# Sliding-window attention: two key blocks folded into one block of 128 columns

## The chip, the cores and the metric

The kernel runs on one core of one Trainium2 chip. The time is what the device takes for one execution, in microseconds (us); three runs of the kernel before gave a median of 1572.53, from 1572.28 to 1574.33. Each engine of the core works through its own queue in order: PE multiplies matrices (PEld loads its weights), DVE and ACT are the vector and the scalar engine, POOL is a second, general engine, and SP issues most DMAs. They wait for each other by semaphores.

## The reference, cut to what matters

One decoder block over 1024 positions of 1024 features: norm, one combined projection, a retention branch and an attention branch in parallel, a gated merge, then a feed-forward part. The change is in the attention branch: 16 query heads of 64 features, 2 key/value heads, a window of 128 positions, and one learned sink logit for each head.

```python
kb = jnp.concatenate([kp[:, :-1], kp[:, 1:]], axis=2)   # the block before, and the block itself
vb = jnp.concatenate([vp[:, :-1], vp[:, 1:]], axis=2)
scores = jnp.einsum('bnqhgd,bnkhd->bnhgqk', qb, kb).astype(jnp.float32) * (d ** -0.5)
rel = C + qi - kj
mask = (rel[None] >= 0) & (rel[None] < WINDOW) & (key_pos >= 0)
scores = jnp.where(mask[None, :, None, None], scores, -1e30)
m = jnp.maximum(jnp.max(scores, axis=-1, keepdims=True), sink)
e = jnp.exp(scores - m)
probs = e / (jnp.sum(e, axis=-1, keepdims=True) + jnp.exp(sink - m))
out = jnp.einsum('bnhgqk,bnkhd->bnqhgd', probs.astype(v.dtype), vb)
```

With C = WINDOW = 128, query row i of a block sees the columns after i of the block before it, and the columns up to i of its own block: together exactly 128, and each column of 0 to 127 once, from one block or the other.

## The kernel before

All activations are held feature by feature in fp32r, most of them as a high and a low part, so that a product takes three matmuls (hi x hi, hi x lo, lo x hi). The attention stage runs from about 98 us to 335 us of the span and is cut into 32 units u = 8g + b: g is a group of four query heads, b a block of 128 queries. The keys stand negated and stacked in `kst`, the values in `vst`, with the high part in columns 0 to 63 and the low part in 64 to 127 of each block and key/value head; `av_evac` writes them from the projection's two halves.

A unit has three parts. `u_scores(u)` multiplies the queries with two key blocks (256 columns; one block for b = 0), two heads to a PSUM bank `s`. DVE adds the mask and takes the row minimum together with the sink in one operation (L464, the scores are negated), ACT takes the exponential with its sum (L467), DVE the reciprocal, and DVE and ACT scale two heads each (L475, L473). POOL copies the sink column into the score tile `sc` first (L452). `u_transpose(u)` transposes the four heads, key block by key block, on PE into banks `pT` (L485), and ACT and DVE write each bank's high part `ph` and low part `pl` (L488, L489). `u_values(u)` multiplies `vst` with `ph` and `pl` of each key block into the bank `pv` (L498, L499); ACT and DVE add the halves (L502 to L505) and write the result over the queries (L507, L508).

The loop at L528 goes through the units as a pipeline: transposes of unit i-1, scores of unit i, a share of other work, then values of unit i-1. The other work is a generator, `Fill`, of plain projections: the query projections of the next group (`quad_q`, tiles `aq`, `wh_aq`, `wl_aq`; rotary work L420 to L429 on DVE and ACT) and sigmoid gates (`gate`, tiles `acc_g`, `wh_g`, `wl_g`). After the last unit the rest of the fill runs (L553), and then the retention-value products begin (tiles `vP`, `va`).

Program order only sets priorities there: a scheduler writes each engine's queue from them, so instructions of units and fill stand in an order of its making, fixed when the program is built. `sc` has two buffers, `ph` and `pl` two, `pT` and `s` two banks each, `pv` one. In the blocks marked `in_order` (the norm ahead of the stage, the vector sums behind it) the order is that of the program.

Of the kernel before, what the change touches and what calls it, by code (L numbers as in the profile page):

```python
# [39 lines left out]
def hybrid_block(ctx: ExitStack, tc: tile.TileContext, x, ln1_g, w_in, b_in, ret_norm_g, w_ret_out,  # L40
# [261 lines left out]
    with tc.tile_pool(name="gt", bufs=1, side="right") as gt, tc.tile_pool(name="w1", bufs=1) as w1:  # L302
        atab = w1.tile([P, 2, S], F32, name="atab")
        nc.sync.dma_start(atab, c_atab.rearrange("z p s -> p z s"))
        amask = w1.tile([P, 256], F32, name="amask")
# [139 lines left out]
        def u_scores(u):  # L445
# [7 lines left out]
            nm = tiny.tile([P, 4], F32, tag="nm", name=f"nm{g}{b}")
            den = tiny.tile([P, 4], F32, tag="den", name=f"den{g}{b}")
            for jp in range(2):
                pt = ps("s", 2, f"s{g}{b}{jp}")
                for jj in range(2):
                    j = 2 * jp + jj
                    o = pt[:, jj * 256:jj * 256 + nk]
                    nc.tensor.matmul(o, Bt[:, jb + j, qc], kst[:, kv, 0, k0:k0 + nk], start=True, stop=False)  # L460
                    nc.tensor.matmul(o, Bt[:, jb + j, qc], kst[:, kv, 1, k0:k0 + nk], start=False, stop=True)  # L461
                for jj in range(2):
                    j = 2 * jp + jj
                    nc.vector.tensor_tensor_reduce(out=sc[:, j, 0:nk], in0=pt[:, jj * 256:jj * 256 + nk], in1=mk,  # L464
                                                   scale=1.0, scalar=nsink[:, 4 * g + j:4 * g + j + 1],
                                                   op0=ALU.add, op1=ALU.min, accum_out=nm[:, j:j + 1])
                    nc.scalar.activation(sc[:, j, 0:nk + 1], sc[:, j, 0:nk + 1], AF.Exp, scale=-1.0,  # L467
# [3 lines left out]
            for j in range(4):  # L471
                if j % 2:
                    nc.scalar.activation(sc[:, j, 0:nk], sc[:, j, 0:nk], AF.Copy, scale=rd[:, j:j + 1])  # L473
                else:
                    nc.vector.tensor_scalar(out=sc[:, j, 0:nk], in0=sc[:, j, 0:nk], scalar1=rd[:, j:j + 1],  # L475
                                            scalar2=None, op0=ALU.mult)

        def u_transpose(u):
            g, b, nk, Bt, jb, qc = geo(u)
            sc = scs.pop(u)  # L480
            phs[u] = []
            for kb in range(nk // P):
                pt = ps("t", 2, f"pT{g}{b}{kb}")
                for j in range(4):
                    nc.tensor.transpose(pt[:, j * P:(j + 1) * P], sc[:, j, kb * P:kb * P + P], ident)  # L485
# [2 lines left out]
                nc.scalar.copy(ph, pt)  # L488
                nc.vector.tensor_tensor(out=pl, in0=pt, in1=f32(ph), op=ALU.subtract)  # L489
                phs[u].append((ph, pl))  # L490

        def u_values(u):
            g, b, nk, Bt, jb, qc = geo(u)
            nkb = nk // P
            pv = ps("pv", 1, f"pv{g}{b}")
            for kb, (ph, pl) in enumerate(phs.pop(u)):
                vb = vst[:, b - nkb + 1 + kb, g // 2, :]
                nc.tensor.matmul(pv, vb, ph, start=(kb == 0), stop=False)  # L498
# [1397 lines left out]
```

## Time and profile before

The profile is of one execution, on its only core. In the views, a row gives line, engine, operation, out<-in by the program's names, shapes and count; then busy us and the mean ns of one; then the engine's idle time ahead of them and what ended it. Timeline rows begin with the start and the time taken, in us.

| | us |
|---|---|
| median of three runs | 1572.53 |
| the profiled execution, whole | 1574.62 |
| its span, first to last instruction | 1572.5 |
| attention stage in it | about 98 to 335 |
| granted TensorE clock, mean | 0.999 of full |

Matmuls overlap in PE's pipeline: a row's duration (389 ns for 512 columns) is longer than the spacing of two that follow each other, so that busy PE time is no measure of how much PE could still take.

### The profile page before, as it was taken

The page shows a single profiled execution, that of the slowest core. Times are in us where ns is not written, and L with a number is a line of the kernel's source. Part 1 is how long each engine was busy: PE and PEld are TensorE (multiplying, and loading weights), DVE is VectorE, ACT ScalarE, POOL GpSimd, SP SyncE. Part 2 cuts the span into 40 slices and gives each one's busy share as a digit, 9 for nine tenths or more (in the row PEclk, how much of TensorE's full clock was granted, in tenths as well). Part 3 has the DMA queues.
Part 4 walks back from the last instruction along what each step waited for, and adds up shares of the span by engine and source line. Part 5 has one row for each costly group of instructions (what it writes and reads, how often), then busy time and mean ns, then how long its engine had stood idle before and what let it go on. Part 6 is the DMA issues. An engine that isn't in the chain of part 4 may idle for free.

```text
span 1572.5 us, 20870 instructions
## 1 busy us (share of the span) xinstructions
PE 1559.8 (99%) x7435; PEld 1297.5 (83%) x7435; DVE 1016.6 (65%) x1809; ACT 732.5 (47%) x1460; POOL 381.8 (24%) x320
## 2 busy tenths in 40 slices
PE   9999999999999999999999999999999999999998
PEld 8887888888888888888888888888888888888886
DVE  6369978777657663787656879444444444678756
ACT  5258877844233334544223366333333333444445
POOL 2000000000045441000021123655555555100001
PEclk9999999999999999999999999999999999999999
DMA  6563754441374454765555502333333333863333
GB/s 203 155 178 118 217 181 148 160 135 41 101 236 148 137 170 164 240 202 165 163 187 186 187 1 78 113 114 105 101 101 106 106 110 101 291 250 84 98 102 126
DMA packets 152581, 228.36 MB, mean 145 GB/s; under 512 B 9307, under 2 KB 81821, under 8 KB 150942
## 3 DMA queue, kind: packets, MB, share of 16 engines
q1 hardware_dynamic: 152476, 227.04, 44.6%
q8 instruction: 58, 0.95, 0.2%
q14 instruction: 45, 0.37, 0.1%
q10 hardware_dynamic: 2, 0.00, 0.0%
HBM read 152.29 MB, written 69.99 MB: 141 GB/s over the span
## 4 chain that ended last, share of the span: by engine, by line
PE 89%; ACT 6%; DVE 3%; issue 1%; DMA 0%; POOL 0%; POOLq 0%; ACTq 0%; DVEq 0%
PE fA L1518 15%; PE fB L1518 8%; PE dA L1820 7%; PE wA L842 7%; PE dxP L1820 6%; PE fC L1518 4%; PE wB L842 3%; PE wo L1352 3%; PE va L687 3%; PE acc_g L158 2%; PE acc_g L159 2%; PE acc_g L160 2%; PE woP L1352 2%; PE vP L687 2%; ACT sc L467 2%; PE acc_ba L159 2%
## 5 line engine op out<-in xcount | busy, mean ns | idle before, releaser
L1820 PE MATMUL dA<-dwP,daP 128*128 128x512 f32 x528 | 120.6, 389 | 0.0
L1820 PEld LDWEIGHTS dA<-dwP,daP 128*128 128x128 f32 x528 | 99.0, 188 | 20.7 <-DVE dwP L134 0.2
L1820 PE MATMUL dxP<-dwP,daP 128*128 128x512 f32 x396 | 90.2, 389 | 0.0
L1820 PEld LDWEIGHTS dxP<-dwP,daP 128*128 128x128 f32 x396 | 74.3, 188 | 15.4
L452 POOL COPY sc<-nsink 128x4 f32<-128x4 f32 x32 | 13.2, 413 | 274.5 <-PE pT L485 157.2
L158 PE MATMUL acc_g<-h,wh_g 128*128 128x512 f32 x192 | 75.4, 393 | 0.1
L159 PE MATMUL acc_g<-h,wh_g 128*128 128x512 f32 x192 | 75.2, 392 | 0.0
L160 PE MATMUL acc_g<-h,wl_g 128*128 128x512 f32 x192 | 75.1, 393 | 0.0
L467 ACT ACTIVATE sc<-sc,nm 128x257 f32<-128x257 f32 (+1 forms) x128 | 62.5, 492 | 27.0 <-DVE nm L464 26.6
L1593 POOL TENSOR_TENSOR xf<-xf 128x512 f32<-128x512 f32 x40 | 64.5, 1611 | 30.3 <-issue 28.8
L1524 POOL TENSOR_TENSOR xf<-xf 128x512 f32<-128x512 f32 x33 | 47.3, 1435 | 58.7 <-ACT xf L1526 26.9
L464 DVE CUSTOM_DVE_ANT_0 sc<-s,amask,nsink 128x256 f32<-128x256 f32 (+1 forms) x128 | 54.0, 460 | 9.8 <-PE s L461 9.5
L134 DVE TENSOR_TENSOR dwP<-wd,dwP 128x512 fp32r<-128x512 f32 x77 | 52.6, 684 | 5.5 <-ACT dwP L131 5.5
L1725 POOL TENSOR_TENSOR rs_f<-tot,mhalf 128x1 f32<-128x1 f32 x8 | 4.9, 607 | 205.4 <-DVE tot L1722 205.4
L131 ACT CAST dwP<-wd 128x512 fp32r<-128x512 f32 x77 | 47.4, 616 | 9.3 <-PE dA L1820 7.1
L131 ACT CAST daP<-daP 128x512 fp32r<-128x512 f32 x42 | 26.0, 621 | 54.0 <-PE dxP L1820 26.7
L158 PE MATMUL acc_bb<-ay,wh_bb 128*128 128x512 f32 x128 | 51.1, 400 | 0.0
L556 POOL TENSOR_TENSOR wr_wp<-wr_wp 128x512 f32<-128x512 f32 x10 | 16.6, 1658 | 140.0 <-DVE w0P L134 122.5
L159 PE MATMUL acc_bb<-ay,wh_bb 128*128 128x512 f32 x128 | 50.3, 393 | 0.0
L160 PE MATMUL aq<-h,wl_aq 128*128 128x512 f32 x128 | 50.2, 392 | 0.0
L159 PE MATMUL aq<-h,wh_aq 128*128 128x512 f32 x128 | 50.2, 392 | 0.0
L158 PE MATMUL aq<-h,wh_aq 128*128 128x512 f32 x128 | 50.2, 392 | 0.0
(826 smaller groups left out, 4374.6 us busy)
## 6 DMA issues: line engine op xcount, KB each, us to landing
act_d<-xf SPq DMA_DIRECT2D x77, 256.0 KB, 2.1
daP<-act_d SPq DMA_DIRECT2D x21, 512.0 KB, 3.6
q_d<-stg SPq DMA_DIRECT2D x8, 1024.0 KB
q<-q_d SPq DMA_DIRECT2D x32, 256.0 KB, 6.2
ay_d<-q SPq DMA_DIRECT2D x8, 1024.0 KB
ay<-ay_d SPq DMA_DIRECT2D x4, 2048.0 KB, 14.2
wr_daP<-act_d SPq DMA_DIRECT2D x14, 512.0 KB, 6.4
wr_g<-in_w_in SPq DMA_DIRECT2D x12, 512.0 KB, 6.0
```

Source lines behind the costliest of these rows:

```text
L131: nc.scalar.copy(hi, raw)
L158: nc.tensor.matmul(pt, hi[:, k, :], xh, start=(k == 0), stop=False)
L159: nc.tensor.matmul(pt, hi[:, k, :], xl, start=False, stop=False)
L160: nc.tensor.matmul(pt, lo[:, k, :], xh, start=False, stop=(k == 7))
L464: nc.vector.tensor_tensor_reduce(out=sc[:, j, 0:nk], in0=pt[:, jj * 256:jj * 256 + nk], in1=mk, scale=1.0, scalar=nsink[:, 4 * g + j:4 * g ...
L467: nc.scalar.activation(sc[:, j, 0:nk + 1], sc[:, j, 0:nk + 1], AF.Exp, scale=-1.0, bias=nm[:, j:j + 1], accum_out=den[:, j:j + 1])
L687: nc.tensor.matmul(vbanks[pr][tt], x_[:, c], w[:, u, :], start=(fresh and k + z == 0), stop=(k == 3 and z == 2), skip_group_check=not fresh)
L842: nc.tensor.matmul(pt, o[:, w, k, :], v, start=(first and k + z == 0), stop=(k == 3 and z == 2), skip_group_check=not first)
L1352: nc.tensor.matmul(bank, v[:, q + u, k, c], w[y][:, k % 2, :], start=(first and z == 0), stop=(last and z == 2), skip_group_check=not tracked)
L1518: nc.tensor.matmul(pt, o[:, w, k, :], v, start=(first and n == 0), stop=(n == 11), skip_group_check=not first)
L1593: nc.gpsimd.tensor_tensor(out=o, in0=a, in1=b, op=op)
L1820: nc.tensor.matmul(banks[tt], a[:, u, c], w[:, v, :], start=(fresh and f + z == 0), stop=(f == NP - 1 and z == 2), skip_group_check=not fresh)
```

## The change

The two key blocks of a query block are folded into one of 128 columns, right behind the scores. Where column c is after row i, the score of the block before is taken; elsewhere the score of the block itself. ACT copies the own block's scores from PSUM into `sc` (two heads at a time), DVE overwrites the columns of the mask with those of the block before (`copy_predicated`), and DVE takes the minimum over 128 columns and the sink (`tensor_reduce`). Exponential, scaling, transposes and the split into `ph` and `pl` then work on 128 columns instead of 256. Units with b = 0 keep the old minimum, with one block's mask.

The values' product has to undo the fold. Blocks alternate: the folded probabilities are multiplied with the even block of the pair, and a masked part of them with the difference of odd and even block. The masked part is made by POOL: `qh` and `ql` are `ph` and `pl` times a mask of zeros and ones, which depends on whether b is odd. So for b > 0 the products stay four: `ph`, `pl` with `vev`, then `qh`, `ql` with `vdf`. `av_evac` writes the even blocks, the odd ones as a scratch, and seven differences of neighbours, each with a high and a low part. `ph`, `pl`, `qh` and `ql` have one buffer each.

```diff
-        vst = w1.tile([P, NB, 2, P], F32R, name="vst")
+        vev = w1.tile([P, NB // 2, 2, P], F32R, name="vev")
+        vdf = w1.tile([P, NB - 1, 2, P], F32R, name="vdf")
+        vodd = w1.tile([P, NB // 2, P], F32, tag="pl", bufs=1, name="vodd")
...
-            nc.scalar.copy(hi, pv)
-            nc.vector.tensor_tensor(out=lo, in0=pv, in1=f32(hi), op=ALU.subtract)
+            pv = p2.rearrange("p (c z f) -> p c z f", c=2, z=2)
+            even = vev[:, half * 2:half * 2 + 2]
+            hl_of(even, pv[:, :, 0].rearrange("p c (v e) -> p c v e", v=2))
+            odd = vodd[:, half * 2:half * 2 + 2, :]
+            nc.scalar.copy(odd, pv[:, :, 1])
+            df = w1.tile([P, 4, 132], F32, tag="sc", bufs=2, name=f"vdf{half}")
+            b0 = half * 4
+            nc.vector.tensor_tensor(out=df[:, 1:3, 0:P], in0=odd[:, 0:1, :].to_broadcast([P, 2, P]), in1=pv[:, :, 0],
+                                    op=ALU.subtract)
+            nc.vector.tensor_tensor(out=df[:, 3, 0:P], in0=odd[:, 1, :], in1=pv[:, 1, 0], op=ALU.subtract)
+            if half:
+                nc.vector.tensor_tensor(out=df[:, 0, 0:P], in0=vodd[:, 1, :], in1=pv[:, 0, 0], op=ALU.subtract)
+            lo = 0 if half else 1
+            hl_of(vdf[:, b0 + lo - 1:b0 + 3], df[:, lo:4, 0:P].rearrange("p c (v e) -> p c v e", v=2))
+
+        def hl_of(o, v):
+            hi, lo = o[:, :, :, 0:64], o[:, :, :, 64:128]
+            nc.scalar.copy(hi, v)
+            nc.vector.tensor_tensor(out=lo, in0=v, in1=f32(hi), op=ALU.subtract)
...
+                jr = slice(2 * jp, 2 * jp + 2)
+                if b > 0:
+                    ptv = pt.rearrange("p (j z s) -> p j z s", j=2, z=2)
+                    nc.scalar.copy(sc[:, jr, 0:P], ptv[:, :, 1])
+                    nc.vector.copy_predicated(sc[:, jr, 0:P], mk.bitcast(U32).rearrange("p (o s) -> p o s", o=1)
+                                              .to_broadcast([P, 2, P]), ptv[:, :, 0])
+                    nc.vector.tensor_reduce(out=nm[:, jr], in_=sc[:, jr, 0:P + 1], op=ALU.min,
+                                            axis=mybir.AxisListType.X)
...
-            for kb in range(nk // P):
-                pt = ps("t", 2, f"pT{g}{b}{kb}")
-                for j in range(4):
-                    nc.tensor.transpose(pt[:, j * P:(j + 1) * P], sc[:, j, kb * P:kb * P + P], ident)
-                ph = w1.tile([P, 512], F32R, tag="ph", bufs=2, name=f"ph{g}{b}{kb}")
-                pl = w1.tile([P, 512], F32R, tag="pl", bufs=2, name=f"pl{g}{b}{kb}")
-                nc.scalar.copy(ph, pt)
-                nc.vector.tensor_tensor(out=pl, in0=pt, in1=f32(ph), op=ALU.subtract)
-                phs[u].append((ph, pl))
+            pt = ps("t", 2, f"pT{g}{b}")
+            for j in range(4):
+                nc.tensor.transpose(pt[:, j * P:(j + 1) * P], sc[:, j, 0:P], ident)
+            ph, pl = (w1.tile([P, 512], F32R, tag=t, bufs=1, name=f"{t}{g}{b}") for t in ("ph", "pl"))
+            nc.scalar.copy(ph, pt)
+            nc.vector.tensor_tensor(out=pl, in0=pt, in1=f32(ph), op=ALU.subtract)
+            phs[u] = [(vev[:, b // 2], ph, pl)]
+            if b > 0:
+                mk = amask[:, (1 + b % 2) * P:(2 + b % 2) * P].rearrange("p (o s) -> p o s", o=1).to_broadcast([P, 4, P])
+                part = []
+                for t, src in (("qh", ph), ("ql", pl)):
+                    o = w1.tile([P, 512], F32R, tag=t, bufs=1, name=f"{t}{g}{b}")
+                    nc.gpsimd.tensor_tensor(out=o.rearrange("p (j q) -> p j q", j=4),
+                                            in0=f32(src).rearrange("p (j q) -> p j q", j=4), in1=mk, op=ALU.mult)
+                    part.append(o)
+                phs[u].append((vdf[:, b - 1], *part))
...
-            for kb, (ph, pl) in enumerate(phs.pop(u)):
-                vb = vst[:, b - nkb + 1 + kb, g // 2, :]
-                nc.tensor.matmul(pv, vb, ph, start=(kb == 0), stop=False)
-                nc.tensor.matmul(pv, vb, pl, start=False, stop=(kb == nkb - 1))
+            parts = phs.pop(u)
+            for n, (vb, *hl) in enumerate(parts):
+                for z, p in enumerate(hl):
+                    nc.tensor.matmul(pv, vb[:, g // 2, :], p, start=(n + z == 0), stop=(n == len(parts) - 1 and z == 1))
...
-    amask = np.where((rel >= 0) & (rel < P), 0.0, 1e30).astype(np.float32)
+    amask = np.concatenate([np.where(col > row, 1e30, 0.0), row > col, row <= col], axis=1).astype(np.float32)
```

The scheduler writes the queues anew, and the names below carry its buffer numbers. First PE, around the values of unit 4 (g = 0, b = 4). Before, its transposes stand a few rows ahead; then fill (L158 to L160, `aq`) and the four products, two for each key block:

```order
L498 MATMUL pv_1347<-ph_1281,vst 128x512
L158 MATMUL aq_1434<-h_111,wh_aq_1418 128x512
L159 MATMUL aq_1434<-h_111,wh_aq_1418 128x512
L160 MATMUL aq_1434<-h_111,wl_aq_1419 128x512
L158 MATMUL aq_1434<-h_111,wh_aq_1418 128x512
L159 MATMUL aq_1434<-h_111,wh_aq_1418 128x512
L499 MATMUL pv_1347<-pl_1282,vst 128x512
L498 MATMUL pv_1347<-ph_1290,vst 128x512
L160 MATMUL aq_1434<-h_111,wl_aq_1419 128x512
L499 MATMUL pv_1347<-pl_1291,vst 128x512
```

Now, in the changed kernel (its line numbers; L509 are the transposes, L159 to L161 the fill, L530 the values), from the last transpose of unit 4 to its last product:

```order
L509 MATMUL pT_1284<-ident,sc_1210 128x128 x4
L159 MATMUL aq_1436<-h_111,wh_aq_1420 128x512
L160 MATMUL aq_1436<-h_111,wh_aq_1420 128x512
L161 MATMUL aq_1436<-h_111,wl_aq_1421 128x512
L159 MATMUL aq_1436<-h_111,wh_aq_1420 128x512
L530 MATMUL pv_1352<-ph_1289,vev 128x512
L160 MATMUL aq_1436<-h_111,wh_aq_1420 128x512
L161 MATMUL aq_1436<-h_111,wl_aq_1421 128x512
L530 MATMUL pv_1352<-pl_1290,vev 128x512
L530 MATMUL pv_1352<-qh_1293,vdf 128x512
L530 MATMUL pv_1352<-ql_1295,vdf 128x512
```

Nine matmuls stand between the last transpose and the product with `ql`, and the products with `pl`, `qh` and `ql` follow each other without fill between them.

Second POOL, in the same part of the stage. Before, there were only copies of the sink column, one for each unit (L452); now (L469 the copy, L519 the masked parts) the copy for unit u+2 stands ahead of the two products of unit u:

```order
L469 COPY sc_1297<-nsink 128x4
L519 TENSOR_TENSOR qh_1206<-ph_1202,amask 128x512
L519 TENSOR_TENSOR ql_1208<-pl_1203,amask 128x512
L469 COPY sc_1377<-nsink 128x4
L519 TENSOR_TENSOR qh_1293<-ph_1289,amask 128x512
L519 TENSOR_TENSOR ql_1295<-pl_1290,amask 128x512
```

Behind the copy for a tile of `sc` (`sc_1377` is unit 6) come the products of an earlier unit (`qh_1293` and `ql_1295` are unit 4).

Third PE late in the stage, from the end of unit 30's products to unit 31's transposes. Before, with gate fill (`acc_g`) around them:

```order
L499 MATMUL pv_3605<-pl_3543,vst 128x512
L485 MATMUL pT_3618<-ident,sc_3546 128x128 x3
L485 MATMUL pT_3627<-ident,sc_3546 128x128
L485 MATMUL pT_3618<-ident,sc_3546 128x128
L485 MATMUL pT_3627<-ident,sc_3546 128x128 x3
L158 MATMUL acc_g_0_3601<-h_110,wh_g_3597 128x512
```

Now, the same place:

```order
L530 MATMUL pv_3541<-pl_3473,vev 128x512
L530 MATMUL pv_3541<-qh_3476,vdf 128x512
L530 MATMUL pv_3541<-ql_3478,vdf 128x512
L509 MATMUL pT_3554<-ident,sc_3480 128x128 x4
L159 MATMUL acc_g_0_3537<-h_110,wh_g_3533 128x512
L160 MATMUL acc_g_0_3537<-h_110,wh_g_3533 128x512
```

Eight transposes became four. Behind them, before and now, stand 21 fill matmuls, and then the last unit's products.

More of the change, by code (lines that the diff above doesn't have):

```diff
@@ L13 @@
 BF16 = mybir.dt.bfloat16
+U32 = mybir.dt.uint32
 AF = mybir.ActivationFunctionType
@@ L448, in u_scores @@
             k0 = (b - 1) * P if b > 0 else 0
-            mk = amask[:, 256 - nk:256]
-            sc = w1.tile([P, 4, 260], F32, tag="sc", bufs=2, name=f"sc{g}{b}")
+            mk = amask[:, 0:P]
+            sc = w1.tile([P, 4, 132], F32, tag="sc", bufs=2, name=f"sc{g}{b}")
             scs[u] = sc
-            nc.gpsimd.tensor_copy(sc[:, :, nk:nk + 1], nsink[:, 4 * g:4 * g + 4].rearrange("p (j o) -> p j o", o=1))
+            nc.gpsimd.tensor_copy(sc[:, :, P:P + 1], nsink[:, 4 * g:4 * g + 4].rearrange("p (j o) -> p j o", o=1))
             nm = tiny.tile([P, 4], F32, tag="nm", name=f"nm{g}{b}")
@@ L461, in u_scores @@
                     nc.tensor.matmul(o, Bt[:, jb + j, qc], kst[:, kv, 1, k0:k0 + nk], start=False, stop=True)
+                jr = slice(2 * jp, 2 * jp + 2)
[6 more added lines that the diff above has]
+                                            axis=mybir.AxisListType.X)
                 for jj in range(2):
                     j = 2 * jp + jj
[L464 to L467, printed above, removed]
+                    if b == 0:
+                        nc.vector.tensor_tensor_reduce(out=sc[:, j, 0:P], in0=pt[:, jj * 256:jj * 256 + P], in1=mk,
+                                                       scale=1.0, scalar=nsink[:, 4 * g + j:4 * g + j + 1],
+                                                       op0=ALU.add, op1=ALU.min, accum_out=nm[:, j:j + 1])
+                    nc.scalar.activation(sc[:, j, 0:P + 1], sc[:, j, 0:P + 1], AF.Exp, scale=-1.0,
                                          bias=nm[:, j:j + 1], accum_out=den[:, j:j + 1])
@@ L472, in u_scores @@
                 if j % 2:
-                    nc.scalar.activation(sc[:, j, 0:nk], sc[:, j, 0:nk], AF.Copy, scale=rd[:, j:j + 1])
+                    nc.scalar.activation(sc[:, j, 0:P], sc[:, j, 0:P], AF.Copy, scale=rd[:, j:j + 1])
                 else:
-                    nc.vector.tensor_scalar(out=sc[:, j, 0:nk], in0=sc[:, j, 0:nk], scalar1=rd[:, j:j + 1],
+                    nc.vector.tensor_scalar(out=sc[:, j, 0:P], in0=sc[:, j, 0:P], scalar1=rd[:, j:j + 1],
                                             scalar2=None, op0=ALU.mult)
@@ L1857, in _tables @@
     rtab = np.stack([np.concatenate([cr, cr]), np.concatenate([-sr, sr])])
-    qi = np.arange(P)[:, None]
-    kj = np.arange(2 * P)[None, :]
-    rel = P + qi - kj
-    amask = np.where((rel >= 0) & (rel < P), 0.0, 1e30).astype(np.float32)
+    row, col = np.arange(P)[:, None], np.arange(P)[None, :]
+    amask = np.concatenate([np.where(col > row, 1e30, 0.0), row > col, row <= col], axis=1).astype(np.float32)
     idx = np.arange(P, dtype=np.float64)
```

7 lines of the change are left out of this document (1 added, 6 removed).

## The prediction

> **What bounds the kernel now.** The page first, for the engine that fills the span and the chain that ends last.
>
> ```profile
> span 1572.5 us, 20870 instructions
> ...
> PE 1559.8 (99%) x7435; PEld 1297.5 (83%) x7435; DVE 1016.6 (65%) x1809; ACT 732.5 (47%) x1460; POOL 381.8 (24%) x320
> ...
> PE 89%; ACT 6%; DVE 3%; issue 1%; DMA 0%; POOL 0%; POOLq 0%; ACTq 0%; DVEq 0%
> ```
>
> TensorE carries the end. The change lies in the attention stage alone, so the next view is busy time by stretch of that stage (columns: stretch, its length, PE, PEld, DVE, ACT, POOL, granted clock, DMA share, GB/s).
>
> ```profile
> 98.00:160.00 62.00, 61.16 (x337) 49.63 (x336) 57.75 (x180) 54.49 (x161) 3.47 (x10) 1.00 0.52 152
> 160.00:206.00 46.00, 45.45 (x239) 36.92 (x238) 40.76 (x114) 39.15 (x105) 3.38 (x7) 1.00 0.63 184
> 206.00:266.00 60.00, 58.70 (x314) 48.89 (x313) 51.90 (x153) 47.50 (x131) 4.12 (x8) 1.00 0.62 203
> 266.00:326.00 60.00, 59.24 (x315) 49.59 (x313) 40.99 (x125) 46.52 (x128) 1.86 (x6) 1.00 0.34 110
> 326.00:359.00 33.00, 33.00 (x148) 27.30 (x147) 25.05 (x27) 8.86 (x18) 0.00 (x0) 1.00 0.49 160
> ```
>
> PE is busy throughout, but in the first stretch DVE is busy 93% and ACT 88%: PE is hardly ahead of them there. POOL is nearly idle. A busy PE hides short holes, because matmuls overlap. So I count the stage's matmuls (97.9 to 335 us) and price them by their spacing when nothing holds them.
>
> ```profile
> L159 PE MATMUL acc_g<-h,wh_g 128*128 128x512 f32 x144 | 56.6, 393 | 0.0
> L160 PE MATMUL acc_g<-h,wl_g 128*128 128x512 f32 x144 | 56.4, 394 | 0.0
> L158 PE MATMUL acc_g<-h,wh_g 128*128 128x512 f32 x143 | 56.4, 394 | 0.1
> L485 PE MATMUL pT<-ident,sc 128*128 128x128 f32 x240 | 35.0, 280 | 2.5 <-ACT sc L473 1.3 <-ACT tm L503 0.5 <-DVE sc L475 0.4
> L460 PE MATMUL s<-kst,q 128*128 128x256 f32 x112 | 29.9, 293 | 0.3 <-DVE nm L464 0.3
> ...
> L160 PE MATMUL aq<-h,wl_aq 128*128 128x512 f32 x64 | 25.3, 396 | 0.0
> ...
> L498 PE MATMUL pv<-ph,vst 128*128 128x512 f32 x60 | 24.2, 404 | 0.4 <-DVE tm L505 0.4
> ```
> ```profile
> 370.01 10.88 PE vP L687 x48
> ```
> ```profile
> 256.89 0.86 PEld L485 LDWEIGHTS pT<-ident,sc 128*128 128x128 f32 x8 [0.34 <-issue]
> ```
>
> Spacings: 10.88/48 = 0.227 us for 512 columns, 0.86/8 = 0.108 for a transpose, about 0.12 for 256 columns of scores (half of 0.227 and a little). The groups aq and pv come in three and two equal parts. 431 + 192 + 120 = 743 wide matmuls make 168.4 us, 240 transposes 25.9, 224 wide and 32 narrow scores some 28; sum 222. The stretch is 237 us: PE works at its peak but for **about 15 us of holes**, made by waits for ACT and DVE.
>
> **The change, part by part.** PE first. Scores keep their 256 columns and values keep four matmuls for each unit with b > 0 (hi and lo of the probabilities, then hi and lo of the masked ones). Only the transposes fall from 8 to 4 in 28 units: 112 x 0.108 = **12.1 us** off PE, all of it on the path.
>
> DVE and ACT, by these rows:
>
> ```profile
> L464 DVE CUSTOM_DVE_ANT_0 sc<-s,amask,nsink 128x256 f32<-128x256 f32 x112 | 49.2, 476 | 1.3 <-PE s L461 1.0
> L489 DVE TENSOR_TENSOR pl<-pT,ph 128x512 fp32r<-128x512 f32 x60 | 40.4, 686 | 1.8 <-ACT ph L488 1.0
> ...
> L508 DVE TENSOR_TENSOR q<-tm,q 128x256 fp32r<-128x256 f32 x32 | 13.3, 417 | 0.9 <-ACT q L507 0.8
> ...
> L475 DVE TENSOR_SCALAR sc<-sc,rd 128x128 f32<-128x128 f32 x8 | 1.9, 282 | 0.1
> ```
> ```profile
> L467 ACT ACTIVATE sc<-sc,nm 128x257 f32<-128x257 f32 x112 | 56.2, 505 | 20.2 <-DVE nm L464 19.8
> L488 ACT CAST ph<-pT 128x512 fp32r<-128x512 f32 x60 | 32.7, 586 | 1.7 <-PE pT L485 1.2
> L473 ACT ACTIVATE sc<-sc,rd 128x256 f32<-128x256 f32 x56 | 25.3, 500 | 1.9 <-DVE rd L470 1.8
> ...
> L507 ACT CAST q<-tm 128x256 fp32r<-128x256 f32 x32 | 13.0, 407 | 2.1 <-DVE tm L505 2.0
> ...
> L467 ACT ACTIVATE sc<-sc,nm 128x129 f32<-128x129 f32 x16 | 6.3, 399 | 6.8 <-DVE nm L464 6.8
> ...
> L473 ACT ACTIVATE sc<-sc,rd 128x128 f32<-128x128 f32 x8 | 2.8, 394 | 0.5 <-DVE rd L470 0.5
> ```
>
> A unit's DVE loses four masked minima (4 x 0.476) and one pl (0.686), 2.6 us; it gains two predicated copies and two minima over 256 columns, which the trace does not show. Bounds: 0.28 (128 columns) to 0.69 (512); I take 0.42, the row for 256 columns: 1.7 us. Net -0.9 us, 28 units: -25 us (bounds -41 to +4). ACT loses 4 x 0.106 on the exponentials, one ph (0.59), and 0.2 on two narrower scalings, and gains two copies of 256 columns at 0.41: -0.4 us, 28 units: -11 us. The score chain gains a hop (PE to ACT to DVE to DVE to ACT). The scores stand a unit or more ahead of their transposes in the order, so I cost the hop at nothing; without that cover it is about 1 us a unit in the first stretch.
>
> POOL is where it turns. It gets two products of 128x512 for each of the 28 units, qh behind ph and ql behind pl, and PE needs both before the unit's last two matmuls. The price of one:
>
> ```profile
> 8.84 2.50 POOL L362 TENSOR_TENSOR wl_ak<-wr_kv,wh_ak 128x512 fp32r<-128x512 f32 x2 [0.89 <-ACT wh_ak L357]
> ```
> ```profile
> 979.75 3.45 POOL L1593 TENSOR_TENSOR xf<-xf 128x512 f32<-128x512 f32 x2
> 980.27 1.78 DVE L134 TENSOR_TENSOR t_3P<-wr_f,t_3P 128x512 fp32r<-128x512 f32 x1
> 981.97 0.68 DVE L1542 TENSOR_TENSOR xf<-fC,p 128x512 f32<-128x512 f32 x1
> ```
>
> [...] One unit with a single bank shows what comes ahead of them:
>
> ```profile
> 209.89 0.60 PE L485 MATMUL pT<-ident,sc 128*128 128x128 f32 x4
> ...
> 210.25 0.36 PE L460 MATMUL s<-kst,q 128*128 128x256 f32 x1
> ...
> 210.47 0.36 ACT L503 COPY tm<-pv 64x256 f32<-64x256 f32 x1
> ...
> 210.86 0.59 ACT L488 CAST ph<-pT 128x512 fp32r<-128x512 f32 x1
> ```
>
> PE went on at 210.25; ph ended at 211.45, 1.2 us later, of which some 0.3 is the tm copy in front. So from the last transpose to ql done: 0.9 to 1.2 plus 2.50 to 3.45, that is **3.4 to 4.65 us**. I take 4.0.
>
> What does PE have to do in between? That is in its order: matmuls behind the last transpose and ahead of ql, times their spacing. In the excerpt of unit 4: four fills, ph, two fills, pl, qh = 9 x 0.227 = 2.0 us. Counted so for each unit u = 8g+b, 19 of the 28 have 4.3 to 6.4 us of cover; ql is hidden there. **Nine have not**: units 1, 2, 4, 5, 6, 7, 15, 21, 22 have 2.5, 2.4, 2.0, 2.3, 2.1, 2.5, 1.1, 2.3, 2.9 us, 20.1 in all. PE takes its queue in order, so ql holds the fills and the next transposes behind it, and ACT and DVE wait for those. 9 x 4.0 - 20.1 = **15.9 us** of new stall (bounds 30.6 - 20.1 = 10.5 and 41.9 - 20.1 = 21.8).
>
> Not all of it is new. These nine units own 9/32 of the 15 us of holes; while PE waits for ql, ACT and DVE catch up, so about 4 us of old holes vanish under the stall (bounds 0 and, with all holes of the first stretch, 6). Of the remaining 11 us of holes the shorter ACT and DVE queues take perhaps a fifth, 2 us (bounds 0 and 5).
>
> [...]
>
> Set-up: the value evacuations (L349, L350, one on ACT and one on DVE each half) become three on ACT and four or five on DVE, beside the first norm and the projections, where
>
> ```profile
> 40.00:76.00 36.00, 36.00 (x180) 30.35 (x179) 14.31 (x22) 11.30 (x19) 0.00 (x0) 1.00 0.46 141
> ```
>
> shows PE full with DVE at 40%. For the second half that hides them; the first half falls among the last norms, on DVE. I take 0.5 us; bounds 0 and 3 (five more DVE operations of about 0.6). The mask's DMA grows by half, long before its use. Behind the attention, from the first retention-value product on, the orders of PE, DVE, ACT and POOL are the same as before, and 120 gate matmuls still stand between the last attention product and that point, over the DVE chain of sums (25.05 busy in the last stretch); no change there.
>
> **Sum**: -12.1 + 15.9 - 4 - 2 + 0.5 = **-1.7 us**. The profiled execution took 1574.6 us around its span of 1572.5; it lies 2 us above the median of the runs, and I put the difference on the median: 1572.5 - 1.7 = 1570.8.
>
> **Rivals.** *The POOL products stay hidden*, because the old holes sit just where ql is late, or ph comes sooner: then the transposes' whole 12.1 and 2 us of holes are won, -13.6, 1559. For it: POOL is idle and DVE and ACT lose work. Against it: 2.50 us for two is the fastest that this trace shows, and unit 4's cover is 2.0 with ph still to come. In between lie shorter chains: 3.4 us gives -7.1, 1565.
>
> [...] Rows 980.27 and 979.75 show both sides paying. A unit's POOL products meet scalings (L475), hi/lo splits (L508, L403) and rotary products (L420 to L425) on DVE. If each of the 56 meets one, at 0.5 us each, 28 us go back onto DVE, more than it saved; then no holes are won (+2) and ql takes the upper bound, 21.8 instead of 15.9: -1.7 + 2 + 5.9 = +6.2, 1578.7. It decides from a chain of about 4.2 us, where the sum crosses zero. A predicated copy at its upper bound works the same way. For it: DVE is 93% busy in the first stretch, where six of the nine units lie. Against it: right behind pl, DVE mostly has PSUM work (predicated copies) and minima.
>
> [...]
>
> *PE's gain is none*, because ACT bounds the stage: it is at 54.49 of 62 in the first stretch and loses 11 us over the stage, so I give it nothing.
>
> **Chances.** Forecast (1565 to 1576) 0.55; hidden products 0.17; port 0.28. The measurement tells about 0.2%, 3.1 us, from no change. Faster by more: 0.17 and 0.2 of the forecast's, 0.37; slower by more: 0.25 of the port's and 0.03, 0.28; between: 0.35. The range runs from 1561 to 1580: it takes in both bounds of the chain and most of both rivals, and leaves the last tenth of each side out.
>
> **What would show it.** Transposes x128; POOL products x56 at 1.25 to 1.75 us; PE waiting for POOL 1 to 2.5 us in the nine units and hardly elsewhere; late units 0.4 us shorter each; the stage's end within 5 us of 335. No PE wait for POOL would make me wrong on the fast side; DVE rows of scalings and splits above 0.7 us on the slow side; PE waits in the late units would break the count of covers.

## The result and the profile after

The changed kernel took **1584.31 us** (median of 4 runs, 1582.45 to 1585.31), the kernel before 1573.42 beside it: ratio 1.0073, 95% interval 1.006 to 1.0085. It is slower by 10.9 us, outside the forecast range (1561 to 1580) and on the other side of the forecast's sign.

The page of the profiled execution (1584.13 us around its span):

```profile
span 1582.3 us, 20602 instructions
...
PE 1555.2 (98%) x7323; PEld 1288.0 (81%) x7323; DVE 1013.4 (64%) x1676; ACT 719.6 (45%) x1492; POOL 452.8 (29%) x376
...
PE 89%; DVE 4%; ACT 4%; POOL 2%; issue 1%; DMA 1%; POOLq 0%; DVEq 0%; ACTq 0%; SPq 0%
```

112 matmuls fewer, all of them transposes, and yet 9.8 us more span. POOL is on the chain now, with 2%. Busy time by stretch of the attention stage, same columns and cuts as before:

```profile
98.00:160.00 62.00, 54.97 (x273) 40.91 (x273) 51.86 (x128) 46.30 (x157) 21.00 (x23) 1.00 0.46 128
160.00:206.00 46.00, 41.95 (x194) 33.90 (x192) 35.79 (x77) 31.89 (x100) 15.17 (x15) 0.89 0.61 178
206.00:266.00 60.00, 55.72 (x278) 44.68 (x275) 48.47 (x111) 42.25 (x130) 21.55 (x19) 1.00 0.59 203
266.00:326.00 60.00, 58.16 (x298) 47.96 (x299) 39.95 (x101) 46.34 (x149) 23.90 (x25) 1.00 0.44 135
```

PE, 61.16 of 62 us busy before, is down to 54.97 in the first stretch, and DVE and ACT are *less* busy as well: none of the three fills the stretch. In the second stretch the granted clock is 0.89. Behind 359 us the traces agree: the last transpose of unit 31 starts 9.5 us later than before (335.4 against 325.9), and the span is 9.8 us longer. So the loss lies in the stage.

To place it, I sum over all matmuls between the last transposes of units 0 and 31 the time from one start to the next. What exceeds the priced spacing (0.227 us for 512 columns, 0.116 for 256, 0.109 for a transpose, 0.058 for 128 columns of scores) is a **hole**. Before: 222.6 us = 208.8 of work + 13.8 of holes. After: 232.9 = 197.5 + **35.4**. Work fell by 11.3, as forecast (the twelfth microsecond went to four wide matmuls that moved in between the two marks); holes grew by 21.7, where the forecast had 9.9.

What the trace says PE waited for in the stage (us in total, times, longest):

```profile
PEld pv L530 <- POOL ql L519: 11.9, 11, 1.4
PE pv L530 <- POOL ql L519: 8.0, 11, 1.0
...
PE pT L509 <- DVE sc L501: 2.9, 4, 1.7
```

The wait for ql is there. The last row, DVE's scaling late for the transposes, was not in the forecast. The groups of DVE and POOL in the stage (busy us, mean ns) show where it comes from:

```profile
L483 DVE COPY_PREDICATED sc<-amask,s 128x256 f32<-128x256 uint32 x56 | 23.1, 438 | 1.4 <-ACT sc L482 1.0
L485 DVE TENSOR_REDUCE nm<-sc 128x2 f32<-128x258 f32 x56 | 22.1, 412 | 0.3
L501 DVE TENSOR_SCALAR sc<-sc,rd 128x128 f32<-128x128 f32 x64 | 19.3, 342 | 0.7
L539 DVE TENSOR_TENSOR q<-tm,q 128x256 fp32r<-128x256 f32 x32 | 17.1, 535 | 1.3 <-ACT q L538 1.2
...
L444 DVE TENSOR_TENSOR stg<-stg 128x512 fp32r<-128x512 f32 x6 | 6.7, 1110 | 0.4 <-ACT stg L443 0.4
L446 DVE TENSOR_TENSOR stg<-stg 128x512 fp32r<-128x512 f32 x6 | 6.2, 1041 | 0.0
```
```profile
L519 POOL TENSOR_TENSOR ql<-pl,amask 128x512 fp32r<-128x512 f32 x28 | 40.0, 1428 | 10.1 <-DVE pl L512 10.0
L519 POOL TENSOR_TENSOR qh<-ph,amask 128x512 fp32r<-128x512 f32 x28 | 37.5, 1339 | 27.0 <-ACT ph L511 27.0
```

The two new DVE operations cost what was assumed (0.42). But the splits of q went from 417 to 535 ns, scalings of 128 columns from 282 to 342, and two of the rotary operations from 687 and 684 to 1110 and 1041. These are means: four of the 64 scalings, started while a product ran, took 0.97 to 1.38 us, and the other 60 took 0.27 to 0.30. The timeline at unit 10 shows how that reaches PE (start, us taken):

```profile
163.69 0.36 ACT L482 COPY sc<-s 128x256 f32<-128x256 f32 x1
...
164.94 1.30 POOL L519 TENSOR_TENSOR qh<-ph,amask 128x512 fp32r<-128x512 f32 x1 [0.45 <-ACT ph L511]
...
165.49 1.29 DVE L444 TENSOR_TENSOR stg<-stg 128x512 fp32r<-128x512 f32 x1
...
166.19 1.74 POOL L519 TENSOR_TENSOR ql<-pl,amask 128x512 fp32r<-128x512 f32 x1
...
166.71 1.77 DVE L446 TENSOR_TENSOR stg<-stg 128x512 fp32r<-128x512 f32 x1
...
168.40 0.41 DVE L539 TENSOR_TENSOR q<-tm,q 128x256 fp32r<-128x256 f32 x1
...
168.74 0.76 DVE L483 COPY_PREDICATED sc<-amask,s 128x256 f32<-128x256 uint32 x2
...
171.74 0.48 DVE L501 TENSOR_SCALAR sc<-sc,rd 128x128 f32<-128x128 f32 x2
...
172.17 0.30 PE L509 MATMUL pT<-ident,sc 128*128 128x128 f32 x1 [1.68 <-DVE sc L501]
```

Unit 10's scores are in `sc` at 164.05, but DVE folds them only at 168.74: it stands in two rotary operations of the next group, each beside a POOL product, which take 3.06 us in place of 1.37. The exponentials and scalings follow, and PE waits 1.68 us. Not all of that wait is POOL's: without POOL's products (the first experiment below) PE waits at the same place too:

```profile
160.24 0.30 PE L509 MATMUL pT<-ident,sc 128*128 128x128 f32 x1 [1.08 <-DVE sc L501]
```

The two operations lost 1.7 us, and the whole interval from unit 9's last transpose to unit 10's grew by 1.2, from 8.0 to 9.2. The same trace shows who holds up whom. Four rotary rows that started just ahead of a product (122.29, 174.28, 246.50 and 259.42 us) kept their 0.68 us, and the product beside them took 1.55 to 1.72 us, where undisturbed ones take 1.27 to 1.30. The ten rotary rows that started behind a product all ended 0.54 to 0.56 us after its end, as if they had begun only then.

The trace shows which of DVE's rows grow. Those of pl (one input in PSUM) that overlap a product took 684 to 694 ns and the minima 401 to 423, where the ones that met no product took 678 to 692 and 403 to 422. The operations with two SBUF inputs grow, rotary rows up to 1.78 us and splits of q up to 1.09, and so do four scalings that started beside a product, up to 1.38.

### The profile page after: what moved, and what is told of

Read it like the earlier page. It is cut to its first block, busy times and chain, and to the rows that moved or that the text cites. A ratio compares the mean times of both kernels' runs of the same rounds, so it can differ in the third digit from the quotient of the medians.

```text
span 1582.3 us, 20602 instructions
## 1 busy us (share of the span) xinstructions
PE 1555.2 (98%) x7323; PEld 1288.0 (81%) x7323; DVE 1013.4 (64%) x1676; ACT 719.6 (45%) x1492; POOL 452.8 (29%) x376
## 4 chain that ended last, share of the span: by engine, by line
PE 89%; DVE 4%; ACT 4%; POOL 2%; issue 1%; DMA 1%; POOLq 0%; DVEq 0%; ACTq 0%; SPq 0%
PE fA L1549 15%; PE fB L1549 8%; PE dA L1851 7%; PE wA L873 7%; PE dxP L1851 6%; PE fC L1549 4%; PE wB L873 3%; PE wo L1383 3%; PE va L718 3%; PE acc_g L159 2%; PE acc_g L160 2%; PE acc_g L161 2%; PE woP L1383 2%; PE vP L718 2%; PE acc_ba L159 2%; PE acc_ba L160 2%
## 5 line engine op out<-in xcount | busy, mean ns | idle before, releaser
L159 PE MATMUL acc_g<-h,wh_g 128*128 128x512 f32 x192 | 77.2, 402 | 1.4 <-ACT wh_g L132 1.4
L160 PE MATMUL acc_g<-h,wh_g 128*128 128x512 f32 x192 | 76.2, 397 | 0.0
L161 PE MATMUL acc_g<-h,wl_g 128*128 128x512 f32 x192 | 75.8, 396 | 0.0
L1624 POOL TENSOR_TENSOR xf<-xf 128x512 f32<-128x512 f32 x40 | 62.4, 1561 | 30.7 <-issue 28.9
L469 POOL COPY sc<-nsink 128x4 f32<-128x4 f32 x32 | 11.5, 359 | 191.1 <-PE pT L509 157.8
L493 ACT ACTIVATE sc<-sc,nm 128x129 f32<-128x129 f32 x128 | 50.4, 396 | 26.6 <-DVE nm L485 20.7
L1038 POOL TENSOR_TENSOR grs<-gve,mhalf 128x2 f32<-128x2 f32 x16 | 11.2, 701 | 145.5 <-DVE gve L1036 145.5
L587 POOL TENSOR_TENSOR wr_f<-wr_f 128x512 f32<-128x512 f32 x20 | 30.6, 1532 | 76.8 <-DVE t_10P L135 8.6
L159 PE MATMUL acc_bb<-ay,wh_bb 128*128 128x512 f32 x128 | 50.9, 399 | 0.0
L159 PE MATMUL aq<-h,wh_aq 128*128 128x512 f32 x128 | 50.4, 394 | 0.0
L160 PE MATMUL acc_bb<-ay,wh_bb 128*128 128x512 f32 x128 | 50.3, 393 | 0.0
L160 PE MATMUL aq<-h,wh_aq 128*128 128x512 f32 x128 | 50.3, 393 | 0.0
```

The costliest lines, as they stand in the source:

```text
L159: nc.tensor.matmul(pt, hi[:, k, :], xh, start=(k == 0), stop=False)
L160: nc.tensor.matmul(pt, hi[:, k, :], xl, start=False, stop=False)
L161: nc.tensor.matmul(pt, lo[:, k, :], xh, start=False, stop=(k == 7))
L493: nc.scalar.activation(sc[:, j, 0:P + 1], sc[:, j, 0:P + 1], AF.Exp, scale=-1.0, bias=nm[:, j:j + 1], accum_out=den[:, j:j + 1])
L1624: nc.gpsimd.tensor_tensor(out=o, in0=a, in1=b, op=op)
```

## The experiments

All times are medians; the kernel before had 1574.1 to 1574.3 beside them. Holes are those between the last transposes of units 0 and 31.

| kernel | us | ratio to before, 95% interval | work + holes, us |
|---|---|---|---|
| before | 1573.42 | | 208.8 + 13.8 |
| changed | 1584.31 | 1.0073 (1.006 to 1.0085) | 197.5 + 35.4 |
| e1_unmasked | 1564.32 | 0.9942 (0.9927 to 0.9957) | 197.5 + 17.5 |
| e2_onlooker | 1576.39 | 1.0019 (1.001 to 1.0028) | 197.5 + 29.5 |
| e3_dve | 1564.34 | 0.9943 (0.9928 to 0.9958) | 199.3 + 17.3 |
| e4_split | 1578.46 | 1.0028 (1.0016 to 1.0041) | 198.0 + 31.4 |
| e6_peorder | 1585.78 | 1.0076 (1.0059 to 1.0092) | 213.6 + 34.0 |
| e7_warm | 1583.55 | 1.0059 (1.0046 to 1.0073) | 199.1 + 35.6 |
| e8_poolcopy | 1569.32 | 0.9972 (0.9962 to 0.9983) | 197.5 + 21.2 |
| e9_dvepsum | 1566.43 | 0.9955 (0.9941 to 0.9968) | 199.3 + 20.3 |
| e10_dve_order | 1593.19 | 1.013 (1.0115 to 1.0145) | 214.5 + 40.7 |
| e11_balance | 1563.97 | 0.9944 (0.9927 to 0.9961) | 199.5 + 17.3 |

### No masked products

```diff
-                for t, src in (("qh", ph), ("ql", pl)):
...
-                phs[u].append((vdf[:, b - 1], *part))
+                phs[u].append((vdf[:, b - 1], ph, pl))
```

> Leaves out the 56 masked products on POOL: the last two matmuls of a unit read ph and pl in place of qh and ql, so the masking of the values is not computed. Fold, score chain, transposes and the order on PE stay those of the changed kernel. In the changed kernel the holes on PE between the first and the last unit's transposes add up to 35.4 us, against 13.7 before. If POOL is the cause (PE waiting for ql, and DVE slowed beside POOL), the holes go back to about 14 us and the time to 1584.3 - 21.7 = 1562.6, between 1559 and 1565. If the longer score chain of the fold (PE to ACT to DVE to DVE to ACT) or the new order on PE is the cause, POOL changes little and the time stays above 1576.

Measured 1564.32, inside the range for POOL as the cause, though with 17.5 us of holes and not about 14. The fold as such is a gain of 10 us; **POOL's 56 products cost 20.0 us** (17.9 by the holes; the rest is the start of the span, where executions differ by some 2 us). DVE's rows are back:

```profile
L501 DVE TENSOR_SCALAR sc<-sc,rd 128x128 f32<-128x128 f32 x64 | 15.5, 283 | 0.7
L532 DVE TENSOR_TENSOR q<-tm,q 128x256 fp32r<-128x256 f32 x32 | 13.3, 417 | 1.3 <-ACT q L531 1.2
...
L444 DVE TENSOR_TENSOR stg<-stg 128x512 fp32r<-128x512 f32 x6 | 4.1, 688 | 0.4 <-ACT stg L443 0.3
L446 DVE TENSOR_TENSOR stg<-stg 128x512 fp32r<-128x512 f32 x6 | 4.1, 688 | 0.0
```

### Products made, but waited for by nobody

```diff
-                phs[u].append((vdf[:, b - 1], *part))
+                phs[u].append((vdf[:, b - 1], ph, pl))
```

> POOL makes qh and ql as in the changed kernel, but nobody waits for them: the last two matmuls of a unit read ph and pl, so the masking of the values is not in the result. PE's order is the same. This keeps POOL's load beside DVE and takes only the wait away. If the wait for ql is the cost, the intervals behind the nine units with short cover (15.5 us of holes, 4.7 before) lose about 11 us: 1573.5, and as in the run without products, 1560 to 1565, if the other holes are its echo as well. If the slower DVE beside POOL is the cost, the rotary rows stay near 1 us in place of 0.68, the large holes at units 10, 11, 16 and 21 stay, and the time is 1578 to 1584.

Measured 1576.39, between the two. Taking away the wait alone gives 7.9 us (5.9 by the holes); POOL's mere running beside DVE costs the other **12.1** (12.0 by the holes). No run has the wait without the load, so this is the split in that order: the load first, the wait on top. The rows of DVE are those of the changed kernel:

```profile
L501 DVE TENSOR_SCALAR sc<-sc,rd 128x128 f32<-128x128 f32 x64 | 19.2, 339 | 0.7
L539 DVE TENSOR_TENSOR q<-tm,q 128x256 fp32r<-128x256 f32 x32 | 17.3, 541 | 1.3 <-ACT q L538 1.2
...
L444 DVE TENSOR_TENSOR stg<-stg 128x512 fp32r<-128x512 f32 x6 | 6.6, 1093 | 0.4 <-ACT stg L443 0.4
L446 DVE TENSOR_TENSOR stg<-stg 128x512 fp32r<-128x512 f32 x6 | 6.3, 1046 | 0.0
```

PE's order is the same in the changed kernel and these two but for one swapped pair here and a dozen rows around unit 4 in the run without products (the interval up to unit 4 has 0.4 us of holes there and 2.3 here, so at most 1.9 of the 12 can be the order's). So their holes can be laid side by side, as time from one unit's last transpose to the next's (us):

| intervals | before | changed | not waited for | no products |
|---|---|---|---|---|
| behind the nine units of short cover | 4.6 | 15.6 | 10.3 | 6.9 |
| ending at units 4, 10, 11, 21 | 2.0 | 14.0 | 13.5 | 6.7 |
| the other 18 | 7.1 | 5.8 | 5.7 | 3.9 |

In the nine, the wait is a good half of what POOL costs. In the four, it is next to nothing: these hold rotary operations beside POOL products (L444 at 127.7, 165.5 and 181.1 us, L446 at 260.0, each 1.3 to 1.8 us long).

The interval up to unit 11 also holds a stretch at half the granted clock: 10.2 us long in the changed kernel and in this run, 3.4 us without products. PE's matmuls that followed each other there without a recorded wait started 3.8, 3.6 and 1.6 us in all later than at the priced spacing. So about 2 of the 12 us show up as a slower PE behind the waits, and not as waits.

### Both products on DVE

```diff
-                    nc.gpsimd.tensor_tensor(out=o.rearrange("p (j q) -> p j q", j=4),
+                    nc.vector.tensor_tensor(out=o.rearrange("p (j q) -> p j q", j=4),
```

> The 56 masked products run on DVE instead of POOL; all is computed. DVE gets 56 x about 0.69 = 38.6 us, and gives back the 16 us by which its rows are longer beside POOL; the chain from ph to ql falls from about 3.4 us to about 2.1. The order on all engines is made anew. If POOL's slowness and the port are the cause and DVE has room, 1565 to 1572. If DVE bounds the stage (it is 84% busy in the first stretch of the changed kernel, and gets 1.4 us a unit), 1585 to 1600.

Measured 1564.34, with all of the computation: 20 us below the changed kernel, 10 below the one before. That is just below the range given for room on DVE. DVE takes 38.3 us on top and is as busy in the first stretch as before the change, yet PE's holes fall to 17.3:

```profile
98.00:160.00 62.00, 59.38 (x304) 46.73 (x302) 57.83 (x147) 51.14 (x169) 3.10 (x10) 1.00 0.53 157
```
```profile
L519 DVE TENSOR_TENSOR ql<-pl,amask 128x512 fp32r<-128x512 f32 x28 | 19.2, 684 | 0.0
L519 DVE TENSOR_TENSOR qh<-ph,amask 128x512 fp32r<-128x512 f32 x28 | 19.1, 684 | 0.0
```

0.68 us each against 1.34 and 1.43 on POOL, and 16 us of lengthened rows saved; a port as such, which the expectation names, is shown by no run. That it equals the kernel without products is not to be read as "DVE work is free": the order was made anew, and the four intervals with rotary work, 6.7 us of holes without products, have 3.0 here, with the granted clock at 1.00 throughout the stage.

### PE in program order

```diff
-        for i in range(NU + 1):
+        with in_order(nc.tensor.engine):
+            for i in range(NU + 1):
```

> The changed kernel, with PE's queue in the stage held to program order: transposes of a unit, scores of the next, fill, values. Then ql has 5.0 to 6.4 us of matmuls in front of it in every unit, and the scores 5.0 us or more to their transposes. POOL's work is the same. If the order's short covers are the cause, PE's waits for POOL (8.0 us in PE's own rows, 11.9 in its weight loads) vanish and the time falls to 1565 to 1573. If DVE's slowing beside POOL is the cause in itself, it falls little, 1578 to 1584. If the fold's score chain needs more than the 5 us, new waits for the scalings appear in most units and the time rises over 1584.

Measured 1585.78, no better. PE's wait for POOL almost vanishes, and waits for the scalings take its place:

```profile
PE pT L509 <- ACT sc L499: 7.8, 3, 3.7
PE pT L509 <- DVE sc L501: 5.2, 3, 4.2
...
PE pv L530 <- POOL ql L519: 1.5, 3, 0.7
```

That alone could be the order's fault as well as POOL's, so the same order was run with DVE's products.

> Both masked products on DVE, and PE's queue in the stage held to program order, so that 5.0 us or more stand behind every unit's transposes; all is computed. With the products on POOL this order removed PE's waits for POOL and won nothing, because PE then waited for the scalings of the units that meet the rotary work. If POOL beside DVE made those scalings late, the order is worth something here: 1555 to 1562. If the program order as such is the worse one for the score chains (scalings needed at the end of each unit, with no unit further back to take the slack), new waits for the scalings come here too, with DVE carrying 38 us more: 1570 to 1585.

Measured 1593.19, above even the worse of the two ranges: with DVE's products this order is 28.9 us slower than the scheduler's. With a unit's scalings always due right behind one unit's work, PE waits for them at many units:

```profile
PE pT L509 <- DVE sc L501: 18.2, 11, 3.7
...
PE pT L509 <- ACT sc L499: 3.4, 9, 1.2
```

So longer covers for ql cannot be had for nothing. How much of the 28.9 us is the order's and how much the 38 us more on DVE meeting it, this pair does not separate, and it says nothing about POOL.

### One product on each

```diff
-                    nc.gpsimd.tensor_tensor(out=o.rearrange("p (j q) -> p j q", j=4),
+                    (nc.gpsimd if t == "qh" else nc.vector).tensor_tensor(out=o.rearrange("p (j q) -> p j q", j=4),
```

> qh stays on POOL, ql goes to DVE; all is computed. POOL's 28 products run beside pl and ql, so the chain behind ph is the longer of POOL's 1.3 us and DVE's pl and ql, about 1.4 us, shorter than the 2.1 us of both on DVE. DVE gets 28 x 0.69 = 19 us in place of 38. If the length of the chain and DVE's load alone were the cost, this is as fast as both on DVE or faster: 1560 to 1565. If POOL's running beside DVE is itself the larger cost (12 us for 56 products by the run where nobody waits for them), half of it stays: 1568 to 1574, ql's row goes from 0.68 towards 1.2 us, and scalings and rotary rows stay lengthened.

Measured 1578.46 (1573.82 to 1580.26, a wide scatter), 14 us above both on DVE and more than either theory gave. Rows with two SBUF inputs are lengthened again (ql 768 ns on the mean and splits of q 512, with both products on DVE 684 and 419); scalings are not (281 in both), but none of the 64 stood beside a product here:

```profile
L519 DVE TENSOR_TENSOR ql<-pl,amask 128x512 fp32r<-128x512 f32 x28 | 21.5, 768 | 0.2
L539 DVE TENSOR_TENSOR q<-tm,q 128x256 fp32r<-128x256 f32 x32 | 16.4, 512 | 1.8 <-ACT q L538 1.7
L501 DVE TENSOR_SCALAR sc<-sc,rd 128x128 f32<-128x128 f32 x64 | 15.3, 281 | 0.6
```

Over the stage that makes some 8 us of DVE time, too little for 14. The order differs too. And the granted clock is at half for 13.7 us of the stage, with both products on DVE never; matmuls without a recorded wait started 5.3 us in all later there than at the priced spacing. How much each has of the 14 us is open.

### A copy instead of a product

```diff
-                    nc.gpsimd.tensor_tensor(out=o.rearrange("p (j q) -> p j q", j=4),
-                                            in0=f32(src).rearrange("p (j q) -> p j q", j=4), in1=mk, op=ALU.mult)
+                    nc.gpsimd.tensor_copy(o, f32(src))
```

> POOL copies ph to qh and pl to ql in place of multiplying by the mask: one operand from SBUF in place of two; the masking of the values is left out. The orders of all engines are those of the changed kernel, and PE waits for ql as there. If it is the second operand that makes POOL slow and shuts DVE out, the copies are shorter than 1.3 us (no row of a 128x512 copy on POOL is there to say how much), DVE's rotary rows go back to 0.68 and its scalings to 0.28, and the time is 1564 to 1570. If any POOL instruction on SBUF data does it, the rows stay as they are and the time is 1578 to 1585.

Measured 1569.32, 5.0 us above the kernel without POOL work. The orders are those of the changed kernel, so the 15 us between the two come from POOL's instructions alone:

```profile
L519 POOL CAST ql<-pl 128x512 fp32r<-128x512 f32 x28 | 18.6, 665 | 18.3 <-DVE pl L512 18.2
L519 POOL CAST qh<-ph 128x512 fp32r<-128x512 f32 x28 | 18.3, 654 | 29.9 <-ACT ph L511 29.9
```
```profile
L446 DVE TENSOR_TENSOR stg<-stg 128x512 fp32r<-128x512 f32 x6 | 4.9, 818 | 0.0
L444 DVE TENSOR_TENSOR stg<-stg 128x512 fp32r<-128x512 f32 x6 | 4.7, 777 | 0.4 <-ACT stg L443 0.4
```

Without the second operand POOL takes 0.66 us in place of 1.34 to 1.43, and the rotary rows lose less, but are not back at 0.68, as the expectation had it: one-operand copies on POOL hold DVE up too, only for a shorter time (L444 and L446 took 0.78 and 0.82 us on the mean, beside the products 1.11 and 1.04). Half of POOL's time cost a quarter of the 20 us; that both the wait and the delay first use up what slack there is would explain it, but was not tested.

### Is it the clock?

```diff
+            for _ in range(15 if u == 10 else 0):
+                nc.tensor.transpose(pt[:, 0:P], ident, ident)
```

(Unit 11's scores were put ahead of unit 10's transposes in the program, as they stood in PE's order anyway.)

> The changed kernel, with 15 additional transposes of the identity on PE (1.6 us) between the scores of unit 11 and the transposes of unit 10, where PE waits 1.68 us for DVE's scaling. Their bank is overwritten by the real transposes. The order of all else on PE is the same. In the changed kernel the granted clock falls to 0.50 soon after that wait, for some 9 us; 12 gate matmuls then stand 0.43 us apart in place of 0.227 and 8 scores 0.21 in place of 0.116, 3.2 us. If the clock falls because of the wait and PE's time at low clock is lost to the end, it stays at 1.00 and the time falls by 2.5 to 3.2 us, to 1581.5. If the next wait comes all the same (DVE is late for unit 11 anyway), the clock may stay up and the time still be 1584; if the clock falls for another reason, it falls here too.

Measured 1583.55, within the scatter of the changed kernel. Busy time by stretch, the changed kernel first, then this one; the number behind POOL's count is the granted clock:

```profile
174.00:184.00 10.00, 8.59 (x25) 6.82 (x26) 10.00 (x15) 5.18 (x13) 3.01 (x2) 0.53 0.73 181
...
214.00:224.00 10.00, 8.93 (x44) 7.10 (x44) 7.63 (x24) 8.01 (x25) 2.01 (x2) 1.00 0.49 149
```
```profile
174.00:184.00 10.00, 7.26 (x28) 5.05 (x29) 9.78 (x18) 5.49 (x16) 3.39 (x1) 1.00 0.74 214
...
214.00:224.00 10.00, 10.00 (x47) 8.55 (x46) 6.84 (x16) 7.31 (x23) 0.19 (x1) 0.88 0.65 211
```

The clock stays up at 174 to 184 us, and unit 11's transposes come 0.7 us sooner behind unit 9's. The rest of the 3.2 us does not come: DVE is busy nearly all of that stretch in both, and PE now waits 0.91 us for unit 10's ql, where it did not wait before. The clock falls instead at 213 and 261 us, 3.4 us each time. So at this place the low clock set little of the pace; what it costs over the stage is not shown, since it fell elsewhere.

### Two tries for more

qh from the transposes' bank, so that it need not wait for ph:

```diff
+                                            in0=(pt if t == "qh" else f32(src)).rearrange("p (j q) -> p j q", j=4), in1=mk, op=ALU.mult)
```

> Both masked products on DVE, qh taken from the transposes' PSUM bank instead of ph (a mask of zeros and ones commutes with the rounding, so all is computed); qh does not wait for ACT's ph then. DVE's load is that of both products on DVE. If DVE's load sets the pace there, 1564 as with both on DVE from ph. If PE's waits for ph, qh and ql set it, the 0.6 us of ph come off the chain where the cover is short: 1560 to 1563.

1566.43: not better, rather 2 us slower; in PE's own rows the waits for ph and the products had been only 1 to 2 us in all. And one of DVE's two scalings on ACT:

```diff
-                if j % 2:
+                if j > 0:
```

> Both masked products on DVE, and one of DVE's two scalings of a unit moved to ACT: 32 x 0.28 = 9 us off DVE, 32 x 0.39 = 12.6 us onto ACT; all is computed. With both products DVE is busy 57.8 of the first 62 us and ACT 51.1. If DVE's load sets the holes that are left (17.3 us), they shrink and the time is 1558 to 1562. If the scalings are late because ACT's chain of exponentials is (each unit's last PE wait is for an ACT scaling), ACT's longer chain makes it 1565 to 1572.

1563.97 against 1564.34: no difference that these runs tell, 9 us less on DVE notwithstanding, with the same 17.3 us of holes; it lies between the two ranges and bears out neither. Neither moves the kernel past both products on DVE.

## Why the prediction was wrong, step by step

**Transposes: right.** Work on PE fell by 11.3 us between the marks, 12.1 forecast, and the intervals behind units 26 to 30 are 0.5 us shorter on the mean, 0.4 forecast.

**Durations: right.** POOL's products took 1.34 and 1.43 us (1.25 to 1.75 forecast), the two new DVE operations 438 and 412 ns (0.42).

**The wait for ql: right in mechanism, too large in size.** From the last transpose (its start and one spacing) to the end of ql it took 3.45 to 3.94 us in the nine units, 3.6 on the mean, where 4.0 was taken. With that, the term is 9 x 3.6 - 20.1 = 12.3, and less the 4 us of old holes under it 8.3; taking the wait alone away gave 7.9 by the times and 5.9 by the holes, 5.3 of them in the nine units. That 8.3 comes so near to the 7.9 is in part luck: the 4 us were an estimate. PE waited for ql in all nine units, and in units 3 and 20 besides, where DVE's late pl had delayed it.

**The step that failed** is the one that kept a DVE slowed beside POOL out of the sum: it was a rival ("port" in the chances), and the argument against it was that "right behind pl, DVE mostly has PSUM work (predicated copies) and minima". That is true of those operations, whose rows did not change: 30 copies that overlap a product took 432 to 448 ns and 31 minima 401 to 423, where those that met none took 411 to 454 and 403 to 422. For minima that was the author's estimate, as no row of before has one beside a POOL product. No run shows a port as such. What the trace of before shows is two POOL products in 3.45 us at 979.75 us, beside a DVE operation on two SBUF tiles that took 1.78 and one with a PSUM input that took 0.68, against 2.50 us for two products at 8.84 us and 0.68 for a DVE operation of the first kind at 971.00. But the products also meet what the scheduler put beside them from other work, the rotary operations of the next group, and the splits of q and scalings of neighbouring units. Rows with and without POOL work (here against the run without products) give 8.7 + 3.8 + 3.8 = 16 us on DVE. The rival's sign came: scalings of up to 1.38 us and splits of q of up to 1.09 us, where above 0.7 was to tell of it. The rival had priced 28 us of DVE time, by an estimate of 0.5 us for each product where these rows make 0.29, and 8 us of end time from it, too little: the run in which nobody waits puts **12.1 us** on it. The load is a term of its own, 12.1 beside 7.9, and not the wait's other end.

**Old holes: wrong in sign.** 2 us were to vanish through shorter DVE and ACT queues. Without any POOL work 17.5 us of holes are left, against 13.8 before, so 3.7 came. Most stand at units 4, 10, 11 and 21, where 2.0 us were before and 6.7 are now. In the trace without products, 4.0 of the 6.7 lie between the transposes of units 10 and 11: PE waits 1.41 us there for ACT to write the high part of a gate's weights (`wh_g`), and the granted clock is at half for 3.4 us. Both products on DVE, in an order of their own, leave 3.0 at the four units, so it goes with the new order rather than with the fold; which rows of the order make it was not tried, nor was the score chain's extra hop, put at nothing, taken out by itself.

**Set-up: right as a nothing.** The last transpose of unit 0 starts at 102.5 us, 103.4 before, and at 100.1 to 101.4 in the runs with the scheduler's own order.

Sum of what was measured: fold -10.0, load on DVE +12.1, wait +7.9, together +10.0, against +10.9 measured directly. The three are differences of neighbouring runs, so their sum is no test; it misses 10.9 only because the kernel before had 1573.42 in that comparison and 1574.3 in the one with the experiments. "ACT bounds the stage" found no support: ACT is at 46.30 of 62 us in the first stretch, and without POOL's products the fold gains 10 us. The range failed because a DVE slowed beside POOL was taken as an alternative that only stretches the wait (5.9 us, and 2 of holes not won); that a late DVE makes PE wait at the transposes, with ql long done, was never worked out.

## What to carry to other kernels

Work put on an idle engine was not free here: DVE's rows grew by 16 us in all, and the time by 12.1 before anything waited for the result. Count which of the busy engine's operations will stand beside it, from anywhere in the order; here the ten rotary rows that started behind a product met 0.57 to 1.23 us that were left of it, and took 0.44 to 1.10 us longer. Price that delay, and add it to the wait for the result. Before moving work to POOL, price the same instructions on DVE: here, each in an order of its own, 38 us more on an engine busy 9 tenths of the time in the first stretch made a kernel 20 us faster than 77 us on an idle one did. An experiment that keeps the load and drops the wait separates the two in one run.

## What was unexpected of the hardware

A scaling has one SBUF operand tensor, and yet it is held up beside POOL's two-operand products: four of 64 took 0.97 to 1.38 us, each ending 0.1 us behind the product it met, which takes the mean from 283 to 342 ns. Beside the one-operand copies only two scalings stood (279 and 288 ns), too few to say whether copies hold them up.

The granted clock of PE fell to half, at 173.2 us, behind short waits alone. Those in the 4 us ahead of it were 0.32, 1.68 (shown above) and 0.27 us; PE was busy about half of the stretch in which it fell, and the clock came back only 10.2 us later:

```profile
170.00:175.00 5.00, 2.71 (x14) 2.00 (x13) 3.37 (x11) 4.24 (x16) 0.80 (x2) 0.82 0.99 274
175.00:180.00 5.00, 3.59 (x11) 2.68 (x11) 5.00 (x6) 2.63 (x4) 1.11 (x1) 0.50 1.11 268
180.00:185.00 5.00, 5.00 (x16) 3.95 (x15) 5.00 (x9) 2.90 (x11) 1.28 (x1) 0.66 0.31 104
```

Matmuls of 512 columns then started 0.43 us apart. In the stage of every run that had low stretches they lasted 3.4, 6.8 or 10.2 us: one, two or three times the same length. The fall at 173.2 us came behind three short waits, 2.27 us in all, within some 4 us, and it did not come there when transposes filled the longest of them (the clock experiment).
